# A hybrid decoder layer in float32: the long convolution as three filters on even and odd tokens, its sums of x by DMA, gates on half tiles, and another scheduling model

## The chip, the cores and the metric

The kernel runs on one core of one Trainium2 chip. The metric is the device time of one execution in microseconds, as the median of several runs. The engines named below are PE (TensorE, matmuls), DVE (VectorE), ACT (ScalarE), POOL (GpSimd) and SP (SyncE); POOL and SP serve here mainly to issue DMA transfers, each from a queue that works in order.

## What is computed

One layer over 1024 tokens of width 1024, all in float32. Cut to what matters:

```python
h = rms_norm(x, g_mix)
z = h @ w_in + b_in                       # 1024 x 7168
va, ga, xb, gb, sa, sb = split(z)         # 1024, 1024, 1536, 1536, 1024, 1024
u = va * sigmoid(ga)
u = causal_depthwise_conv(u, conv_a_w, conv_a_b)      # width 31
u = silu(layer_norm(u));  y_a = u @ w_a_out
v = causal_depthwise_conv(xb, conv_b_w, conv_b_b)     # width 4
r, i = sigmoid(block_diag(v, w_a)), sigmoid(block_diag(v, w_x))   # 16 heads of 96
v = linear_recurrence(exp(-8 r softplus(-lam)), ...)
y_b = (v * gelu(gb)) @ w_b_out
x = x + (sigmoid(sa) * y_a + sigmoid(sb) * y_b) @ w_o
x = x + square(relu(rms_norm(x, g_mlp) @ w_1)) @ w_2
out = rms_norm(x, g_final)
```

## The kernel before

Channels lie on the 128 partitions and tokens along the free dimension in the first stages. Each float32 product is made of three matmuls on operands split into a high part (a rounded copy, made by ACT) and a low part (the rest: made by a DVE subtraction, or, in `split_dma`, L64, by a negated copy on ACT and a DMA that adds the source to it, issued from POOL's queue). A 128 x 1024 tile of activations comes from the pool `acts` (`T`, 35 buffers).

*First stage.* Chunks of 128 output channels of `z` are made by `zchunk` (L377): two 512-token halves, 48 matmuls of 512 columns each, into a PSUM tile `ps` (three buffers of 128 x 1024). The order is fixed by the loop at L554: three `xb` chunks (`xb_chunk`, for the first four passes), then a `va` and a `ga` chunk (`va_pair`, chunks z0 to z7 and z8 to z15 in the trace), and after each chunk one step of the recurrence branch (`rnn_steps`). `xb_chunk` reads PSUM on ACT (L396) and makes the short convolution. `rnn_gates` (L436) makes two gate products of a head in one 128 x 1024 PSUM tile `ps2`, of which there is a single buffer, and ACT reads it with a sigmoid (L448). `va_pair` makes `u` from two PSUM tiles: sigmoid on ACT (L500), product on DVE (L501). `conv` (L505) is the long convolution of one chunk of `u`: a first product on ACT, then 30 `scalar_tensor_tensor` instructions on DVE, each of which adds one shifted tap to the same tile `acc`. The result is stored (`yd`) and summed into `ysum` for the layer norm: for chunk 0 by a copy on ACT (L521), afterwards on DVE (L523). The table `CONVS` says after which `va` pair a convolution is written: 0 to 4 in the first stage; 5 to 7 come in the z stage.

*Sums of x.* `x_sums` (L538), called twice (for column blocks `c2` 0 and 1), makes four differences of blocks of x for the Strassen-Winograd form of the next stage: four loads, four DVE subtractions, then for each a high copy on ACT (L550) and a low part on DVE (L552).

*z stage* (L569 to L697). The other 28 chunks of `z` (`gb`, `sa`, `sb`) are made in 14 pairs with seven products each (`zseq`: pairs of (i, p)), 12 matmuls a product, into PSUM banks `z_ia`, `b`, `e`, `f`. `z_lhs` makes the left operands `zo` (p = 7 and 3 on ACT and DVE; the others by `split_dma`), `z_step` the products and what reads them.

*Later.* The two output products `yb` and `ya` with the layer norm between (`layer_norm_steps`, taken at j = 1 and 4 of the `yb` loop), the products with the gates `sa` and `sb` (L777, L790), the output projection, and the MLP in Strassen-Winograd form. These stages are the same in both kernels but for the two lines shown below.

The order on each engine is set by a scheduler: it takes the instructions as written, with priorities (`tc.high_priority()`; the convolution's taps have the lowest, `-LOWP`), weighs them with a model of time, and writes one fixed order for each engine. Each engine then works strictly in that order and waits on semaphores. The stages inside `tc.manual_schedule` (the first chunks, the MLP) keep the order as written on ACT, DVE and PE.

Of the kernel before, what the change touches and what calls it, by code (L numbers as in the profile page):

```python
# [9 lines left out]
F32 = mybir.dt.float32  # L10
# [15 lines left out]
CONVS = {0: 0, 1: 1, 2: 2, 3: 3, 5: 4}  # L26
# [4 lines left out]
def trunk_kernel(ctx: ExitStack, tc: tile.TileContext, x, xt_in, vecs, w_in, w_a_out, w_b_out,  # L31
# [186 lines left out]
    def x_spread(hf):  # L218

        rb[hf] = rb["tile"][:, HALVES[hf]]  # L220
# [43 lines left out]
    c4 = sm[:, 7, :]  # L264

# [34 lines left out]
    with tc.manual_schedule(engines={mybir.EngineType.Activation, mybir.EngineType.DVE,  # L300
# [16 lines left out]
        rb["tile"] = PS("rb", "ps2")  # L317
# [47 lines left out]
        decay()  # L365

# [69 lines left out]
    def rnn_gates(n):  # L436
        g, hh = divmod(n, 4)
        vh, vl = parts.pop(n)
        gh, gl = gws[n]
        for gi in range(2):  # L440
            ps = PS(f"rg{n}_{gi}", "ps2")
            for hf in range(2):
                o, hs = ps[:HD, HALVES[hf]], HALVES[hf]
                nc.tensor.matmul(o, gh[:, gi, :], vh[:, hs], start=True, stop=False)
                nc.tensor.matmul(o, gl[:, gi, :], vh[:, hs], start=False, stop=False)
                nc.tensor.matmul(o, gh[:, gi, :], vl[:, hs], start=False, stop=True)  # L446
            a = H(f"g{n}_{gi}")
            nc.scalar.activation(a, ps[:HD, :], AF.Sigmoid, bias=(ba_c, bx_c)[gi][:, n:n + 1])  # L448
# [44 lines left out]
    def va_pair(j):  # L493
        psv = zchunk(VA + j)
        step()
        psg = zchunk(GA + j)
        step()
        u = T(f"u{j}")
        with tc.high_priority():
            nc.scalar.activation(u, psg, AF.Sigmoid, bias=bin_c[:, GA + j:GA + j + 1])  # L500
            nc.vector.scalar_tensor_tensor(u, psv, bin_c[:, VA + j:VA + j + 1], u,  # L501
                                           ALU.add, ALU.mult)
        ut[j] = u

    def conv(j):  # L505
        u = ut.pop(j)
        acc = T(f"y{j}")
# [5 lines left out]
        nc.scalar.activation(acc, u, AF.Identity, scale=tap(0), bias=cab_c[:, j:j + 1])  # L513
        with tc.high_priority(-LOWP):
            for d in range(1, WA):
                nc.vector.scalar_tensor_tensor(acc[:, d:S], u[:, 0:S - d], tap(d), acc[:, d:S],  # L516
                                               ALU.mult, ALU.add)
            nc.sync.dma_start(yd[j], acc)
            if j == 0:
                ysum.append(T("ysum"))  # L520
                nc.scalar.activation(ysum[0], acc, AF.Copy)  # L521
            else:
                nc.vector.tensor_tensor(ysum[0], ysum[0], acc, ALU.add)  # L523
# [13 lines left out]

    def x_sums(c2):  # L538
        q = {}
        for n, (hf, kk) in {12: (1, 0), 11: (0, 0), 22: (1, 1), 21: (0, 1)}.items():  # L540
            q[n] = T(f"xs{n}_{c2}")
            nc.sync.dma_start(q[n], xu[hf, 2 * kk + c2])
        sub = nc.vector.tensor_tensor
        sub(q[11], q[12], q[11], ALU.subtract)
        sub(q[12], q[22], q[12], ALU.subtract)
        sub(q[22], q[22], q[11], ALU.subtract)
        sub(q[21], q[21], q[22], ALU.subtract)
# [16 lines left out]
    for _ in rnn_it:  # L564
        pass
    x_sums(1)


# [118 lines left out]
    for n, (i, p) in enumerate(zseq):  # L687
# [8 lines left out]
        if p == 4 and i in (0, 2, 5):  # L696
            conv({0: 5, 2: 6, 5: 7}[i])  # L697
# [72 lines left out]
    for j in range(8):  # L770
# [7 lines left out]
        if j in (1, 4):  # L778
# [5 lines left out]
    for j in range(8):  # L784
# [5 lines left out]
        nc.vector.tensor_tensor(sa, ps, sa, ALU.mult)  # L790
# [653 lines left out]
```

## Time and profile before

| | |
|---|---|
| median of 3 runs | 1662.33 us (1661.87 to 1665.65) |
| the profiled execution, its own time | 1662.79 us |
| its span in the profile | 1661.0 us |
| mean granted clock of TensorE | 0.983 |
| PE, DVE, ACT, POOL busy | 96%, 70%, 52%, 12% of the span |
| DMA moved | 297.02 MB, mean 179 GB/s |

Busy time by slices of a fortieth of the span (41.5 us), in tenths:

```
PE   8979899997899999989999999999999999999997
DVE  6784999999989995325533224875555367888888
ACT  5537577672755655624453314664444457555552
PEclk9989899998899999999999999999999999999999
```

In the rows quoted below, "L516 DVE ... y<-u,vec,y 128x1009" names the line of the kernel, the engine, output and inputs by tile name, and shape; "[9.25 <-ACT xb L396]" is the time for which the engine stood idle before the instruction and what ended that wait; a line L92 is the helper `mm3`, which makes most matmuls, L66 to L68 the helper `split_dma`.

### The profile page before, as it was taken

The page shows a single profiled execution, that of the slowest core. Times are in us where ns is not written, and L with a number is a line of the kernel's source. Part 1 is how long each engine was busy: PE and PEld are TensorE (multiplying, and loading weights), DVE is VectorE, ACT ScalarE, POOL GpSimd, SP SyncE. Part 2 cuts the span into 40 slices and gives each one's busy share as a digit, 9 for nine tenths or more (in the row PEclk, how much of TensorE's full clock was granted, in tenths as well). Part 3 has the DMA queues.
Part 4 walks back from the last instruction along what each step waited for, and adds up shares of the span by engine and source line. Part 5 has one row for each costly group of instructions (what it writes and reads, how often), then busy time and mean ns, then how long its engine had stood idle before and what let it go on. Part 6 is the DMA issues. An engine that isn't in the chain of part 4 may idle for free.

```text
span 1661.0 us, 18664 instructions
## 1 busy us (share of the span) xinstructions
PE 1588.0 (96%) x6910; PEld 1291.0 (78%) x6910; DVE 1155.5 (70%) x1341; ACT 870.9 (52%) x1135; POOL 201.4 (12%) x268
## 2 busy tenths in 40 slices
PE   8979899997899999989999999999999999999997
PEld 6867677785677777868888888788888888888886
DVE  6784999999989995325533224875555367888888
ACT  5537577672755655624453314664444457555552
POOL 0000000000233333301121100000000001111110
PEclk9989899998899999999999999999999999999999
DMA  9657778765588777847577543442233478988862
GB/s 363 159 135 173 194 198 215 207 184 178 132 232 215 209 203 191 228 143 215 140 204 182 140 154 99 133 159 101 102 126 111 139 257 220 225 215 216 223 131 101
DMA packets 97130, 297.02 MB, mean 179 GB/s; under 512 B 11360, under 2 KB 12896, under 8 KB 97040
## 3 DMA queue, kind: packets, MB, share of 16 engines
q1 hardware_dynamic: 63408, 195.46, 35.3%
q0 software_dynamic: 33488, 100.12, 28.0%
q8 instruction: 54, 0.88, 0.2%
q14 instruction: 36, 0.29, 0.0%
q10 hardware_dynamic: 144, 0.26, 0.0%
HBM read 144.02 MB, written 54.53 MB: 120 GB/s over the span
## 4 chain that ended last, share of the span: by engine, by line
PE 73%; DVE 14%; DMA 6%; issue 4%; ACT 3%; POOL 0%; SPq 0%; DVEq 0%; POOLq 0%; ACTq 0%
PE d L1228 14%; PE yb L92 7%; DVE y L516 7%; PE z L92 6%; PE ya L92 5%; PE o L827 3%; PE e L1343 2%; PE keep L1228 2%; PE o L92 2%; DMA zo<-zw 2%; PE z L257 2%; DMA zo<-zs 1%; DVE g L474 1%; DMA hg<-hgd 1%; DVE v L404 1%
## 5 line engine op out<-in xcount | busy, mean ns | idle before, releaser
L516 DVE SCALAR_TENSOR_TENSOR y<-u,vec,y 128x1009 f32<-128x1009 f32 (+22 forms) x240 | 299.8, 1264 | 6.1 <-ACT y L513 2.6
L92 PE MATMUL z<-xh,win_h 128*128 128x512 f32 x400 | 127.2, 399 | 15.8 <-ACT xb L396 9.2
L92 PE MATMUL z<-xl,win_h 128*128 128x512 f32 x400 | 126.1, 396 | 0.0
L1240 DVE TENSOR_TENSOR acc<-acc,d 128x1024 f32<-128x1024 f32 x72 | 87.8, 1219 | 33.4 <-PE d L1228 32.7
L92 PEld LDWEIGHTS z<-xh,win_h 128*128 128x128 f32 x400 | 76.7, 193 | 34.1 <-ACT xb L396 9.7
L92 PE MATMUL z<-xh,win_l 128*128 128x512 f32 x400 | 94.8, 389 | 0.0
L92 PEld LDWEIGHTS z<-xl,win_h 128*128 128x128 f32 x400 | 76.8, 192 | 17.1
L92 PEld LDWEIGHTS z<-xh,win_l 128*128 128x128 f32 x400 | 75.1, 188 | 15.7
L67 POOL DMA_DIRECT2D win_l<-win_raw x25 | 21.7, 869 | 332.5 <-ACT win_l L66 273.5
L961 ACT ACTIVATE o<-s 128x512 fp32r<-128x512 f32 x64 | 38.1, 621 | 32.7 <-DVE s L953 28.5
L961 ACT ACTIVATE o<-w_raw 128x512 fp32r<-128x512 f32 x40 | 25.0, 624 | 51.2 <-DVE o L875 50.8
L404 DVE SCALAR_TENSOR_TENSOR v<-xb,vec,v 128x1023 f32<-128x1023 f32 (+2 forms) x36 | 45.6, 1277 | 8.8 <-ACT v L399 8.7
L68 ACT ACTIVATE win_h<-win_raw 128x1024 fp32r<-128x1024 f32 x25 | 26.3, 1056 | 43.7 <-PE z L92 37.3
L67 POOL DMA_DIRECT2D zo<-zw x42 | 37.1, 883 | 90.7 <-ACT zo L66 88.5
L448 ACT ACTIVATE g<-rg,vec 96x1024 f32<-96x1024 f32 x32 | 35.6, 1111 | 21.4 <-PE rg L446 14.6
L875 DVE TENSOR_TENSOR o<-s,o 128x512 fp32r<-128x512 f32 x64 | 42.4, 684 | 5.9 <-ACT o L961 5.8
L777 DVE TENSOR_TENSOR m<-yb,sb 128x1024 f32<-128x1024 f32 x8 | 9.8, 1222 | 52.7 <-PE yb L92 52.7
L859 DVE TENSOR_TENSOR x<-xr,o 128x1024 f32<-128x1024 f32 x8 | 9.6, 1218 | 52.2 <-PE o L827 37.7
L67 POOL DMA_DIRECT2D db_1l<-wr x7 | 6.1, 873 | 327.1 <-ACT db_1l L66 304.5
L790 DVE TENSOR_TENSOR sa<-ya,sa 128x1024 f32<-128x1024 f32 x8 | 9.8, 1225 | 43.9 <-PE ya L92 43.9
L118 ACT ACTIVATE xn<-x 128x1024 f32<-128x1024 f32 x8 | 8.5, 1057 | 58.8 <-DVE x L859 58.8
L92 PE MATMUL ya<-suh,wa_h 128*128 128x512 f32 x128 | 39.1, 389 | 0.0
(1577 smaller groups left out, 4599.1 us busy)
## 6 DMA issues: line engine op xcount, KB each, us to landing
fr<-fd SPq DMA_DIRECT2D x32, 512.0 KB, 5.7
wr<-in_w_dram SPq DMA_DIRECT2D x32, 512.0 KB, 5.9
w_raw<-in_w_dram SPq DMA_DIRECT2D x31, 512.0 KB, 3.7
zw<-in_w_in_dram SPq DMA_DIRECT2D x28, 512.0 KB, 4.7
win_raw<-in_w_in_dram SPq DMA_DIRECT2D x25, 512.0 KB, 4.9
win_l<-win_raw POOLq DMA_DIRECT2D x25, 512.0 KB, 4.8
zo<-zw POOLq DMA_DIRECT2D x42, 256.0 KB, 3.6
fd<-fa SPq DMA_DIRECT2D x16, 512.0 KB, 3.3
```

Source lines behind the costliest of these rows:

```text
L67: nc.gpsimd.dma_start(l, src, accum_op=ALU.add)
L92: nc.tensor.matmul(ps[:, HALVES[hf]], a, b[hf], start=i == 0, stop=i == len(todo) - 1)
L257: nc.tensor.matmul(z0[i][:, HALVES[hf]], w0[i][w][:, k, :], xpart(a, hf, k), start=k == 0 and which == "hh", stop=k == 7 and which == "hl" ...
L404: nc.vector.scalar_tensor_tensor(v[:, d:S], a[:, 0:S - d], cbw_c[:, w * 12 + t:w * 12 + t + 1], v[:, d:S], ALU.mult, ALU.add)
L448: nc.scalar.activation(a, ps[:HD, :], AF.Sigmoid, bias=(ba_c, bx_c)[gi][:, n:n + 1])
L516: nc.vector.scalar_tensor_tensor(acc[:, d:S], u[:, 0:S - d], tap(d), acc[:, d:S], ALU.mult, ALU.add)
L827: nc.tensor.matmul(ps[:, HALVES[hf]], tok(a, k, t), wo[k][b][:, HALVES[hf]], start=k == 0 and b == 0 and n == 0, stop=k == 7 and b == 1)
L875: tt(l, src, h.bitcast(F32), ALU.subtract)
L961: nc.scalar.activation(o[:, 0], src, AF.Copy)
L1228: nc.tensor.matmul(o, a, b, start=n == 0 and (p != 1 or g == 0), stop=n == len(todo) - 1, skip_group_check=p == 1 and g > 0)
L1240: tt(acc[p, q2], acc[p, q2], ps, ALU.add)
L1343: nc.tensor.matmul(o, a, b, start=n == 0, stop=n == len(todo) - 1)
```

## The change

1. *Convolution.* `u` is written with the even tokens in the first half and the odd tokens in the second. The 31 taps fall into an even filter (16 taps) and an odd one (15). The product of the two-phase filter is made of three filters on 512 tokens: the even taps on the even tokens (`p0`), the odd taps on the odd tokens (`p1`), and the sums of neighbouring taps (`csum`) on the sum of even and odd tokens (`p2`), from which `p0` and `p1` are then subtracted for the odd outputs; `p1`, shifted by one, is added to `p0` for the even outputs. `y` and `ysum` stay in that order; the product with `sa` puts `ya` back.
2. *Sums of x.* ACT negates a block in place and a DMA from POOL's queue adds the other block. `x_sums` is split into the sums and `x_parts`; the second call of the sums moves to j = 6.
3. *Gates.* Each half of a gate product has a PSUM tile of its own, one bank, two buffers; ACT reads each half with high priority. The 128 x 1024 tile with the tag `ps2` of the first pool goes.
4. *Places.* Convolutions 0 to 3 in the first stage (after pairs 0, 1, 2, 4), 4 to 7 in the z stage (after pairs 0, 1, 4, 7). `ysum`'s first copy moves to DVE. The first layer norm step is taken at j = 2.
5. *Scheduler.* The scheduler weighs the instructions with its other model of time (`schedule_with_timeline_sim`), so the order on every engine outside the manual stages can differ.

```diff
-CONVS = {0: 0, 1: 1, 2: 2, 3: 3, 5: 4}
+CONVS = {0: 0, 1: 1, 2: 2, 4: 3}
+    def PS2(name):
+        return pp.tile([P, HS], F32, tag="half", name=name, bufs=2)
...
+        nc.vector.tensor_scalar(cab2, cab_c, 2.0, None, ALU.mult)
+        pairs = caw[:, 8:].rearrange("p (i o j) -> p i o j", o=2, j=8)
+        nc.vector.tensor_tensor(csum, pairs[:, :, 0, :], pairs[:, :, 1, :], ALU.add)
...
-            ps = PS(f"rg{n}_{gi}", "ps2")
-            for hf in range(2):
-                o, hs = ps[:HD, HALVES[hf]], HALVES[hf]
+            a = H(f"g{n}_{gi}")
+            for hf, hs in enumerate(HALVES):
+                ps = PS2(f"rg{n}_{gi}{hf}")
+                o = ps[:HD, :]
...
-            nc.scalar.activation(a, ps[:HD, :], AF.Sigmoid, bias=(ba_c, bx_c)[gi][:, n:n + 1])
+                with tc.high_priority():
+                    nc.scalar.activation(a[:, hs], o, AF.Sigmoid,
+                                         bias=(ba_c, bx_c)[gi][:, n:n + 1])
...
+            uv = u.rearrange("p (o n) -> p o n", o=2)
+            nc.scalar.activation(uv, psg.rearrange("p (n o) -> p o n", o=2), AF.Sigmoid,
+                                 bias=bin_c[:, GA + j:GA + j + 1])
+            nc.vector.scalar_tensor_tensor(uv, psv.rearrange("p (n o) -> p o n", o=2),
+                                           bin_c[:, VA + j:VA + j + 1], uv, ALU.add, ALU.mult)
...
-        nc.scalar.activation(acc, u, AF.Identity, scale=tap(0), bias=cab_c[:, j:j + 1])
+        nc.scalar.activation(p0, xe, AF.Identity, scale=tap(0), bias=bias)
+        nc.scalar.activation(p1, xo, AF.Copy, scale=tap(1))
         with tc.high_priority(-LOWP):
-            for d in range(1, WA):
-                nc.vector.scalar_tensor_tensor(acc[:, d:S], u[:, 0:S - d], tap(d), acc[:, d:S],
-                                               ALU.mult, ALU.add)
+            nc.vector.tensor_tensor(xs, xe, xo, add)
+            nc.vector.tensor_scalar(p2, xs, taps(0), cab2[:, j:j + 1], ALU.mult, add)
+            for k in range(1, NE):
+                for o, a, c in ((p0, xe, tap(2 * k)), (p2, xs, taps(k)),
+                                (p1, xo, tap(2 * k + 1) if k < NE - 1 else None)):
+                    if c is not None:
+                        nc.vector.scalar_tensor_tensor(o[:, k:], a[:, 0:HS - k], c, o[:, k:],
+                                                       ALU.mult, add)
+            nc.vector.tensor_tensor(p2, p2, p0, sub)
+            nc.vector.tensor_tensor(p2, p2, p1, sub)
+            nc.vector.tensor_tensor(p0[:, 1:], p0[:, 1:], p1[:, 0:HS - 1], add)
             nc.sync.dma_start(yd[j], acc)
             if j == 0:
                 ysum.append(T("ysum"))
-                nc.scalar.activation(ysum[0], acc, AF.Copy)
+                nc.vector.tensor_copy(ysum[0], acc)
...
+        for n in (11, 12):
             q[n] = T(f"xs{n}_{c2}")
+            nc.sync.dma_start(q[n], blk[n])
+        for n, src, b in ((11, 11, 12), (12, 12, 22), (22, 11, 22), (21, 22, 21)):
+            if n not in q:
+                q[n] = T(f"xs{n}_{c2}")
+            nc.scalar.activation(q[n], q[src], AF.Copy, scale=-1.0)
+            nc.gpsimd.dma_start(q[n], blk[b], accum_op=ALU.add)
...
         if j == 5:
             x_sums(0)
-    for _ in rnn_it:
-        pass
-    x_sums(1)
+            x_parts(0)
+        elif j == 6:
+            for _ in rnn_it:
+                pass
+            x_sums(1)
+    x_parts(1)
...
-        if p == 4 and i in (0, 2, 5):
-            conv({0: 5, 2: 6, 5: 7}[i])
+        if p == 4 and i in (0, 1, 4, 7):
+            conv({0: 4, 1: 5, 4: 6, 7: 7}[i])
...
-        if j in (1, 4):
+        if j in (2, 4):
             next(ln_it, None)
...
-        nc.vector.tensor_tensor(sa, ps, sa, ALU.mult)
+        sav = sa.rearrange("p (n o) -> p o n", o=2)
+        nc.vector.tensor_tensor(sav, ps.rearrange("p (o n) -> p o n", o=2), sav, ALU.mult)
...
-    with _tile.TileContext(nc) as tc:
+    with _tile.TileContext(nc, schedule_with_timeline_sim=True) as tc:
```

More of the change, by code (lines that the diff above doesn't have):

```diff
@@ L218, in x_spread @@
     def x_spread(hf):
-        rb[hf] = rb["tile"][:, HALVES[hf]]
+        rb[hf] = PS2(f"rb{hf}")
         for i in range(4):
@@ L264, in trunk_kernel @@
     c4 = sm[:, 7, :]
+    csum = cp.tile([P, WA // 2, 8], F32, name="csum")
+    cab2 = cp.tile([P, 8], F32, name="cab2")
     def decay():
```

29 lines of the change are left out of this document (15 added, 14 removed).

## The prediction

> **What bounds the kernel now.** I read the page first, then busy time by stage, then the waits of PE, then the timelines around its longest waits, and the order in which each built program places its instructions on an engine. Page, busy shares:
>
> ```profile
> span 1661.0 us, 18664 instructions
> PE 1588.0 (96%) x6910; PEld 1291.0 (78%) x6910; DVE 1155.5 (70%) x1341; ACT 870.9 (52%) x1135; POOL 201.4 (12%) x268
> ```
>
> PE is busy for all but 73 us. The windows (busy time of an engine, instructions in brackets, then granted clock, DMA share and GB/s) say where those lie:
>
> ```profile
> 120.00:180.00 60.00, 53.54 (x206) 40.60 (x207) 35.05 (x33) 43.35 (x44) 2.61 (x3) 0.87 0.72 190
> 180.00:240.00 60.00, 60.00 (x264) 48.16 (x263) 58.16 (x53) 45.24 (x45) 3.48 (x4) 1.00 0.75 180
> 360.00:420.00 60.00, 43.63 (x174) 34.58 (x173) 59.57 (x52) 18.29 (x21) 3.15 (x4) 0.88 0.55 179
> 540.00:600.00 60.00, 58.30 (x256) 47.29 (x255) 56.79 (x63) 38.20 (x65) 20.02 (x27) 1.00 0.77 204
> 600.00:660.00 60.00, 55.41 (x232) 44.09 (x231) 41.95 (x46) 32.97 (x58) 18.95 (x26) 0.97 0.78 206
> 780.00:840.00 60.00, 60.00 (x263) 48.99 (x261) 29.80 (x21) 28.92 (x30) 9.73 (x13) 1.00 0.50 129
> ```
>
> A full window holds 264 matmuls (0.227 us each). From 780 on PE is full and the change touches little there, so those 880 us stay. What can be won lies before: the first stage (to 404 us) and the z stage (to some 710), where VectorE is full as well (59.57 of 60 at 360). A stop costs more than itself: in 120 to 180 PE was busy 53.54 us for 206 matmuls worth 46.8, at a clock of 0.87. The three stops that matter, as the timeline of PE has them:
>
> ```profile
> 120.12 1.22 PE L92 MATMUL z<-xh,win_h 128*128 128x512 f32 x2 [9.25 <-ACT xb L396]
> 169.43 0.74 PE L444 MATMUL rg<-vh,rgh 96*96 96x512 f32 x1 [5.14 <-ACT g L448]
> 391.10 1.22 PE L92 MATMUL z<-xh,win_h 128*128 128x512 f32 x2 [5.85 <-ACT u L500]
> ```
>
> **Part 1: the first sum `ysum` leaves ScalarE.** Timelines of ScalarE and VectorE (start, duration):
>
> ```profile
> 110.91 1.06 ACT L66 ACTIVATE win_l<-win_raw 128x1024 fp32r<-128x1024 f32 x1 [2.52 <-PE z L92]
> 118.01 1.06 ACT L521 ACTIVATE ysum<-y 128x1024 f32<-128x1024 f32 x1 [6.04 <-DVE y L516]
> 118.97 1.10 ACT L396 ACTIVATE xb<-z,vec 128x1024 f32<-128x1024 f32 x1
> 90.72 27.25 DVE L516 SCALAR_TENSOR_TENSOR y<-u,vec,y 128x1014 f32<-128x1014 f32 x21
> ```
>
> ScalarE works in order. The copy to `ysum` waits until VectorE's convolution 0 is done, and behind it stands the read of `xb` that frees the PSUM tile PE waits for. Now the copy is VectorE's; in the new order `xb` follows that win_l directly. It starts at 111.9 and ends at 113.0, and PE, which stopped at 120.12 - 9.25 = 110.87, stops 2.1 us: 7.1 won. The cold restart goes mostly too:
>
> ```profile
> 120.00:130.00 10.00, 9.88 (x31) 7.56 (x32) 7.52 (x7) 7.87 (x9) 0.00 (x0) 0.71 0.66 190
> 390.00:400.00 10.00, 8.90 (x30) 7.17 (x31) 9.89 (x9) 1.04 (x1) 0.00 (x0) 0.72 0.96 389
> ```
>
> 31 matmuls are worth 7.0 us and took 9.88: 2.8 lost here, of which I give back 2.4. Part 1: +9.5 (7.1 to 10).
>
> **Part 2: convolution as three filters.** What an instruction costs VectorE is its step to the next start, not its duration:
>
> ```profile
> 384.60 1.25 DVE L516 SCALAR_TENSOR_TENSOR y<-u,vec,y 128x994 f32<-128x994 f32 x1
> 385.77 1.22 DVE L547 TENSOR_TENSOR xs<-xs,xs 128x1024 f32<-128x1024 f32 x1
> 20.59 0.74 DVE L227 SCALAR_TENSOR_TENSOR xc<-xc,vec,rb 128x512 f32<-128x512 f32 x1
> 21.25 0.68 DVE L232 TENSOR_TENSOR xl<-xc,xh 128x512 fp32r<-128x512 f32 x1
> 21.86 0.74 DVE L227 SCALAR_TENSOR_TENSOR xc<-xc,vec,rb 128x512 f32<-128x512 f32 x1
> ```
>
> A tap followed by other work steps 1.17; in the chain above, each tap on the sum of the one before, 27.25 / 21 = 1.30. At 512 wide a tap steps 0.66 and a tensor_tensor 0.61. Before: 30 taps, 35 us interleaved to 39 in a chain. After: 15 + 15 + 14 = 44 taps on three sums in turn, so none waits for its neighbour, 44 x 0.655 = 28.8; xs, the first product and three closing additions 5 x 0.61 = 3.0; together 31.8. That is 3 to 7 us less each, and 8 fewer 1024-wide subtractions (part 4). No trace row has three sums in turn; bounds are 0.61 and the full 0.74 a tap (29.9 and 35.6 us). I take 0.655, the row of the same form.
>
> The Trainium skill, "VectorE: DVE Perf Modes", section "The DRAIN you can't avoid", speaks against this part: the next instruction starts only when the pipe has emptied, chaining cannot skip that, so the count of instructions should be kept low. By that rule a tap costs its whole 0.74 and a convolution 35.6, and almost nothing is won. The trace agrees for dependent taps only (a step of 1.30); an instruction that depends on nothing just written starts before the former has ended (1.17 against 1.25).
>
> What the time gains: between `u0` (first gated product) and `u7` the built orders hold 133 convolution instructions before, 165 us by the steps above (1.24 each), and 199 now, 133 us (0.67 each, the wide `ysum` among them). VectorE so has some 36 us of slack before `u7` (with part 4) and PE is the bound of the first stage: the gain is PE's stops, counted in the other parts, not these 36 us. Two short stops of 0.75 and 1.7 us behind late VectorE results I count at +1 (0 to 2.4).
>
> **Part 3: gates in halves.** PE's waits, in total, times, longest, and the forms:
>
> ```profile
> PE rg L444 <- ACT g L448: 7.1, 4, 5.1
> L448 ACT ACTIVATE g<-rg,vec 96x1024 f32<-96x1024 f32 x32 | 35.6, 1111 | 21.4 <-PE rg L446 14.6 <-DMA g<-g 5.9 <-ACT u L500 0.8
> L893 ACT ACTIVATE hq<-tr_m,vec 128x512 f32<-128x512 f32 x16 | 9.8, 695 | 0.0
> L448 ACT ACT_TABLE_LOAD x9 | 11.5, 1283 | 0.2
> ```
>
> 64 half reads at 0.695 are 44.5 us for 35.6: 9 more on ScalarE, which has 15 us free in 180 to 240. PE now waits for half a tile. But the long wait came of tables and scan work queued ahead of gate 4, and in the new order two tables, a root and a win_l (2 x 1.28 + 2 x 1.05) still stand between gates 3 and 4: about 3 us remain. +3 (-3 to +9, cold restart included).
>
> **Part 4: the sums of x by DMA.** Before, ScalarE's copies of the sums wait for VectorE, and `u6` waits behind them:
>
> ```profile
> 384.72 1.06 ACT L550 ACTIVATE xs6h<-xs 128x1024 fp32r<-128x1024 f32 x1 [9.25 <-DVE xs L546]
> 389.93 1.11 ACT L500 ACTIVATE u<-z,vec 128x1024 f32<-128x1024 f32 x1
> xs<-xu SPq DMA_DIRECT2D x8, 512.0 KB, 6.2
> win_l<-win_raw POOLq DMA_DIRECT2D x25, 512.0 KB, 4.8
> zo<-zs POOLq DMA_DIRECT2D x28, 256.0 KB, 3.8
> L67 POOL DMA_DIRECT2D zo<-zw x42 | 37.1, 883 | 90.7 <-ACT zo L66 88.5 <-PE z13f L637 1.4 <-issue 0.4
> ```
>
> This is the stop of 5.85 at 391.10, and 30 matmuls worth 6.8 took 8.9 after it: 8 us in all. Now a chain takes its place, on the same in-order ScalarE: load (6.2), negate (1), accumulate (0.9 to issue on POOL's queue, 4.8 to land), negate, accumulate, then the copies, then `u6`. Counted from the end of chunk z13, with the load issued 1 us before it: xs11 lands at 12, xs22 at 19, xs21 at 26, `u6` done at 28 and its VectorE part at 30. PE has z6, z14 and z7 in hand (3 x 48 x 0.227 = 32.7) before it needs that tile: the chain is covered by 3 us. Behind it on POOL's queue stand win7_l and win15_l, landing at 20 and 35 and wanted at 29 and 40. +8 (0 where landings take 2 us more).
>
> **Part 5: into the z stage.** Last matmuls of z15, `u7`, the low parts zo2_7 and, ten pairs later, zo12_7, and zo2_7's matmuls on the chain that ended last:
>
> ```profile
> 400.55 3.79 PE L92 MATMUL z<-xh,win_l 128*128 128x512 f32 x16
> 406.67 1.28 DVE L501 SCALAR_TENSOR_TENSOR u<-z,vec,u 128x1024 f32<-128x1024 f32 x1
> 450.88 0.69 DVE L617 TENSOR_TENSOR zo<-zs,zo 128x512 fp32r<-128x512 f32 x1
> 659.37 0.68 DVE L617 TENSOR_TENSOR zo<-zs,zo 128x512 fp32r<-128x512 f32 x1
> 459.03 2.72 PE z2f L637 x12
> ```
>
> Before, z15's end (404.3) to z2f is 54.7 us. After, ScalarE reaches zo0_1 behind the second chain, so PE stands some 8 us there where it stood 11 in several stops; but convolutions 4 and 5 now both sit ahead of zo2_7: 52 taps and the like (33 us), 4 wide subtractions (4.6) and 19 half-wide ones (11.6), 49 us against 16 x 1.19 + 8 x 1.14 + 11.6 = 40 before, which took 43. With the same 3.5 of waits z2f comes 57 us after z15. -2 (-8 to +8).
>
> The z stage itself: a pair takes (659.37 - 450.88) / 10 = 20.85 us before, where PE needs 7 x 12 x 0.227 = 19.1 and VectorE, with 8 to 12 half-wide instructions and 10 to 11 taps, 17 to 20; now it is 18 taps of 0.655, 17 to 19. But PE's stops go on after 600 us, where VectorE has slack. 0 (-20 to +15, rivals).
>
> **Part 6: strided reads.** Even and odd tokens are sorted as ScalarE and VectorE read PSUM; no row has such a read. Between no cost and as much again as an unstrided one (1.1 each, the `u` row above), only `u7`'s two lie on the path: -1 (-2 to 0). The closing products with `sa` hide under full PE. The Trainium skill, "SBUF — State Buffer", section "Door 1: The DMA port swizzle", has lines of 8 bytes in PSUM, two values, and a price for every crossing, which would be the doubling; no row here shows it.
>
> **Sum.** 9.5 + 1 + 3 + 8 - 2 + 0 - 1 = 18.5. The profiled execution took 1662.79 (span 1661.0), the median of the runs is 1662.33, so it stands for them: 1662.8 - 18.5 = 1644.
>
> **Rivals.** (a) *The z stage runs better too.* If less VectorE work brings 20.85 to 19.6 over 12 pairs, 15 more: 1629. For it: VectorE full until 600. Against it: the stops after. (b) *The new fixed order starves the z stage.* The built order puts zo_6's negation behind the z_b copy, itself behind the end of z_a; before it stood ahead. From a negation to PE's use:
>
> ```profile
> 545.61 0.63 ACT L66 ACTIVATE zo<-zw 128x512 fp32r<-128x512 f32 x1 [1.72 <-PE z6f L637]
> 552.66 0.73 PE L637 MATMUL z6a<-xh,zo 128*128 128x512 f32 x2 [1.70 <-DMA zo<-zw]
> ```
>
> That is 7.05 us, now begun 1.4 after z_a's end (two half-wide reads of 0.695), against 30 matmuls or 6.8 us that PE has in hand: 1.65 lost a pair, 20 over 12, and 4 more at zo1_6, which stands behind a read that waits for z0e: 1668. That is the point from which it decides; at a trip of 8 us it loses 2.6 a pair and gives 1644 + 31 + 4 = 1679. Against it: without a queue on POOL the trip is 0.6 + 0.9 + 3.8 = 5.3 us, and zo_2, late in this row, has two matmuls more of cover. (c) *The chain of part 4 is not covered.* With 2 to 3 us more a landing the 8 of part 4 and 6 to 8 at `u7` go: 1660, no change. (d) *A tap pays its whole 0.74:* 4 convolutions x 3.8 use up 15 of the 36 us of slack, and 52 x 0.085 = 4.4 come on the path in part 5: 1649. For it: chained taps do; against it: the steps of 0.66. It is what the Trainium skill's rule of part 2 would make. That the gates or filters do not do what they say I see no sign of: the built program holds the same 6873 matmuls.
>
> **How the numbers follow.** Forecast 0.52; (a) 0.17; (b) 0.14, a third of it short of 1668; (c) 0.08; (d) 0.09. A measurement here tells 0.3%, 5 us, from no change: faster means under 1657. Faster is the forecast less 0.02, (a) and (d): 0.76; slower two thirds of (b) and a little: 0.11; same the rest, 0.13. Range 1625 to 1668: (a) and the upper ends of parts 3 and 5 below, (b) up to 1668 above.
>
> **What would show it.** Part 1: no stop over 3 us near 111. Part 2: a convolution alone on VectorE in 31 to 33 us. Part 3: gate waits halved. Part 4: no wait of `xs6h` longer than its landing with PE stopped behind `u6`. Part 5: z2f 55 to 58 us after z15. It is wrong if PE's idle before 710 us has not fallen, or if waits for zo in the z stage exceed 20 us.

## The result: 16 us slower, and the profile after

The changed kernel takes 1678.2 us (median of 4 runs, 1676.91 to 1679.08) where the kernel before takes 1662.24 in the same comparison (4 runs): a ratio of 1.0091, 95% interval 1.0073 to 1.0108. The forecast was 1644. The profiled execution took 1677.35 us, with a span of 1675.6.

The page of the changed kernel, busy shares:

```profile
span 1675.6 us, 18924 instructions
PE 1588.4 (95%) x6910; PEld 1291.3 (77%) x6910; DVE 1114.5 (67%) x1488; ACT 886.3 (53%) x1184; POOL 205.9 (12%) x276
```

VectorE lost 41 us of work, as meant, and PE's work is the same to 0.4 us. So PE's idle time grew. The windows answer to those of before (busy time and instructions of PE, PEld, DVE, ACT, POOL, then granted clock, DMA share, GB/s):

```profile
120.00:180.00 60.00, 50.54 (x204) 38.19 (x203) 36.67 (x39) 47.75 (x56) 2.58 (x3) 0.89 0.77 210
180.00:240.00 60.00, 55.25 (x242) 43.97 (x241) 52.92 (x68) 43.19 (x49) 3.44 (x4) 1.00 0.61 149
360.00:420.00 60.00, 42.92 (x175) 34.08 (x174) 42.83 (x48) 29.09 (x31) 10.28 (x12) 0.87 0.86 226
540.00:600.00 60.00, 55.19 (x230) 43.66 (x229) 50.93 (x80) 36.34 (x62) 18.83 (x26) 0.97 0.76 203
```

VectorE is no longer full between 360 and 420 (42.83 where it had 59.57), and PE is no better off there: 42.92 for 43.63. From 180 to 240, where PE was full, it now does 242 matmuls instead of 264. So the amount of VectorE's work was not what held PE in these stages. The timeline of PE, its longest stops, and its waits in total (us, times, longest):

```profile
112.38 0.73 PE L95 MATMUL z<-xh,win_h 128*128 128x512 f32 x2 [2.15 <-ACT xb L403]
157.99 0.74 PE L452 MATMUL rg<-vh,rgh 96*96 96x512 f32 x1 [5.52 <-ACT g L456]
164.12 0.74 PE L452 MATMUL rg<-vh,rgh 96*96 96x512 f32 x1 [3.26 <-ACT g L456]
389.23 6.22 PE L95 MATMUL z<-xh,win_l 128*128 128x512 f32 x16 [3.97 <-DMA win_l<-win_raw]
419.50 0.79 PE L683 MATMUL z0a<-xh,zo 128*128 128x512 f32 x1 [12.89 <-ACT zo L71]
```

```profile
PE rg L452 <- ACT g L456: 18.6, 6, 5.5
PE z0a L683 <- ACT zo L71: 12.9, 1, 12.9
```

The stop of 9.25 at 120 us became 2.15, as forecast. In its place stand 18.6 us of waits at the gates (7.1 before) and 12.9 at the start of the z stage (3.8 before; from the end of z15 to z2f PE stands 19.9 us in all, for 12.8). Where the two executions part is read from the timelines of PE: the end of the last z15 matmul, and the first matmuls of z2f, yb and d (us from the start).

| | z15 ends | z2f | yb | ya ends | d | last work |
|---|---|---|---|---|---|---|
| before | 404.3 | 458.9 | 709.3 | 939.1 | 1347.7 | 1657.9 |
| after | 406.6 | 471.1 | 720.8 | 945.5 | 1353.8 | 1672.2 |

So 2.3 us are lost in the first stage and 9.2 more by the start of `yb`, all of them between the end of z15 and z2f (from there to `yb` it is 249.7 us for 250.5 before); 5.1 come back between yb and ya (1.8 of them at the waits for `hgh`; the rest I did not follow); and 8.2 are lost after d, in a stage that the prediction had taken as untouched. The last stage, after and then before (timelines of PE and VectorE: the stops of PE's last products, and the first and the last read of the last product `e`):

```profile
1615.25 0.49 PE L1390 MATMUL e<-lb11h,la21h 128*128 128x512 f32 x1 [1.39 <-ACT la21h L1170]
1617.87 0.50 PE L1275 MATMUL d<-db_4h,da_4h 128*128 128x512 f32 x1 [1.89 <-DVE acc L1287]
1631.34 1.28 DVE L1401 TENSOR_TENSOR y<-acc,e 128x512 f32<-128x512 f32 x2
1663.98 2.48 DVE L1401 TENSOR_TENSOR y<-acc,e 128x512 f32<-128x512 f32 x4 [0.55 <-PE e L1390]
```

```profile
1618.21 1.27 DVE L1354 TENSOR_TENSOR y<-acc,e 128x512 f32<-128x512 f32 x2
1652.64 0.69 DVE L1354 TENSOR_TENSOR y<-acc,e 128x512 f32<-128x512 f32 x1
```

Before, VectorE reads the first tile of `e` at 1618.2, between two folds of `acc`; now all but two of the 16 folds of both halves stand ahead of it in VectorE's order, the first read is 13 us later, PE stops twice, and four half reads are left over when PE is done. This code (`last_part`, `fold`, `finish`) did not change. It is written behind the manual stages of the MLP, so the scheduler places it, and its model of time is the only part of the change that reaches it.

### The profile page after: what moved, and what is told of

It reads as the page before. It is cut to its first block, busy times and chain, and to the rows that moved or that the text cites. A ratio compares the mean times of both kernels' runs of the same rounds, so it can differ in the third digit from the quotient of the medians.

```text
span 1675.6 us, 18924 instructions
## 1 busy us (share of the span) xinstructions
PE 1588.4 (95%) x6910; PEld 1291.3 (77%) x6910; DVE 1114.5 (67%) x1488; ACT 886.3 (53%) x1184; POOL 205.9 (12%) x276
## 4 chain that ended last, share of the span: by engine, by line
PE 62%; issue 11%; DMA 8%; ACT 4%; DVE 3%; POOL 1%; SPq 0%; POOLq 0%; ACTq 0%; DVEq 0%
PE d L1275 13%; PE ya L95 5%; PE yb L95 4%; PE o L874 3%; PE e L1390 3%; PE z L95 3%; PE keep L1275 2%; PE o L95 2%; DMA zo<-zs 2%; DMA zo<-zw 1%; DMA g<-g 1%; PE o L898 1%; DMA yn<-yd 1%; DMA win_l<-win_raw 1%; DMA wb2a_raw<-in_w_b_out_dram 1%
## 5 line engine op out<-in xcount | busy, mean ns | idle before, releaser
L95 PE MATMUL z<-xh,win_l 128*128 128x512 f32 x400 | 99.2, 401 | 4.0 <-DMA win_l<-win_raw 4.0
L548 DVE SCALAR_TENSOR_TENSOR y<-u,vec,y 128x498 f32<-128x498 f32 (+14 forms) x120 | 86.5, 740 | 0.3 <-ACT y L539 0.3
L548 DVE SCALAR_TENSOR_TENSOR yt<-u,vec,yt 128x499 f32<-128x499 f32 (+13 forms) x112 | 83.0, 741 | 0.0
L548 DVE SCALAR_TENSOR_TENSOR y<-yt,csum,y 128x499 f32<-128x499 f32 (+13 forms) x112 | 82.9, 740 | 0.0
L456 ACT ACTIVATE g<-rg,vec 96x512 f32<-96x512 f32 x64 | 41.3, 678 | 42.2 <-PE rg L454 17.3
L452 PE MATMUL rg<-vh,rgh 96*96 96x512 f32 x64 | 27.9, 435 | 18.7 <-ACT g L456 18.6
```

The costliest lines, as they stand in the source:

```text
L95: nc.tensor.matmul(ps[:, HALVES[hf]], a, b[hf], start=i == 0, stop=i == len(todo) - 1)
L456: nc.scalar.activation(a[:, hs], o, AF.Sigmoid, bias=(ba_c, bx_c)[gi][:, n:n + 1])
L548: nc.vector.scalar_tensor_tensor(o[:, k:], a[:, 0:HS - k], c, o[:, k:], ALU.mult, add)
```

## The experiments

All times are medians beside runs of the kernel before on the same chip (1662.1 to 1663.2 in these comparisons). A kernel's own runs spread over 3 to 16 us, so each ratio comes with its 95% interval; a difference of some 3 us between two of these kernels is at the limit of what they can tell.

Two theories came first. **T1**: the order that the scheduler's other model writes costs the time, and the parts themselves gain. **T2**: the parts cost it under any order.

### The model of time alone, the parts alone

The changed kernel with the old model, and the kernel before with the new one:

```diff
-    with _tile.TileContext(nc, schedule_with_timeline_sim=True) as tc:
+    with _tile.TileContext(nc) as tc:
```

> The changed kernel with everything but the scheduler's other model of time. Theory T1 (the order that the new model writes is what costs): the parts bring most of what was forecast, 1645 to 1655 us; ScalarE no longer keeps the read of u7 behind the last negation of the second chain of sums, PE's stop at z0a falls from 12.9 to under 5 us, and the last stage runs as before (8 us back). Theory T2 (the parts themselves cost it: the chain of sums by DMA on an in-order ScalarE, and halves of gates, under any order): only the last stage's 8 us come back, 1667 to 1672 us, with z0a still stopping for over 10 us.

> The kernel before with the scheduler's other model of time and nothing else. T1: slower, 1670 to 1680 us: 8 to 10 us in the last stage (PE's matmuls of the last product stop again and end 15 us later than before) and 4 us or more ahead of it. T2: the last stage's 8 us alone, 1668 to 1672, and nothing lost ahead of 700 us.

Measured: 1672.3 us for the parts under the old model (ratio 1.0064, 1.0052 to 1.0076) and 1697.4 for the new model alone (1.0202, 1.0189 to 1.0215). Both theories hold a part. The new model alone costs 34.5 us, more than either foresaw; from d to the end it takes 319.8 us against 310.2, and nearly three quarters of the loss lie ahead of that. Its window after z15 has VectorE full and PE at a clock of 0.80:

```profile
420.00:480.00 60.00, 44.89 (x164) 35.08 (x164) 60.00 (x62) 25.88 (x40) 8.12 (x11) 0.80 0.44 110
```

But the parts under the old model are 9.4 slower than the kernel before, too, though the last stage is back at 310.2, and PE still stands 13.5 us at z0a, as T2 said. So T1 alone falls.

Then the filters alone (the edits of `conv`, of `u`, of the product with `sa`, and `ysum` on VectorE; places, sums, gates and model as before), and the changed kernel with VectorE's sums of x:

> The kernel before with parts 1 and 2 alone (three filters, the first sum copied on VectorE), its own model of time and its own places of the convolutions. By the prediction's terms 9.5 and 1 us less, and up to 15 less in the z stage if VectorE bounds it: 1637 to 1652. If the filters bring nothing because PE bounds that stage: 1652. If neither (a tap at 512 wide pays its whole 0.74 us and VectorE is the bound from u7 on): 1655 to 1662.

```diff
-            nc.scalar.activation(q[n], q[src], AF.Copy, scale=-1.0)
-            nc.gpsimd.dma_start(q[n], blk[b], accum_op=ALU.add)
+        sub(q[11], q[12], q[11], ALU.subtract)
+        sub(q[12], q[22], q[12], ALU.subtract)
+        sub(q[22], q[22], q[11], ALU.subtract)
+        sub(q[21], q[21], q[22], ALU.subtract)
```

> The changed kernel with the sums of x formed by VectorE as before (no chain of accumulating DMAs) and all else as changed, the new model of time too. T1: the model still places the work badly, 1670 to 1680. T2: the stop of 12.9 us at z0a goes and VectorE gets 8 wide subtractions back, 1662 to 1669, with u7 read right after z15 ends.

Measured: 1663.6 (1.0006, 0.9995 to 1.0016), so parts 1 and 2 bring nothing, which is slower than every expectation (the highest ended at 1662); and 1675.0 (1.0071, 1.0059 to 1.0083), 3 less than the changed kernel, with intervals that overlap. That second run is as T1 said and not as T2 said. In it the read of `u7` comes right behind z15 (404.1 us), and PE stands at the start of the z stage all the same:

```profile
412.05 0.79 PE L672 MATMUL z0a<-xh,zo 128*128 128x512 f32 x1 [8.01 <-ACT zo L71]
421.71 0.79 PE L672 MATMUL z1a<-xh,zo 128*128 128x512 f32 x1 [8.01 <-ACT zo L71]
450.49 0.80 PE L672 MATMUL z1b<-xs6h,zo 128*128 128x512 f32 x1 [4.91 <-ACT zo L71]
```

### Where the gain of part 1 goes

In the filters-alone kernel the stop at 120 is gone. Its timeline of PE has another, and behind it stand its window from 140 to 175 us and the groups of table loads on ScalarE in that window:

```profile
170.91 0.74 PE L449 MATMUL rg<-vh,rgh 96*96 96x512 f32 x1 [13.65 <-ACT g L453]
```

```profile
140.00:175.00 35.00, 20.15 (x82) 14.83 (x81) 17.20 (x17) 31.76 (x30) 1.74 (x2) 0.79 0.64 167
```

```profile
L469 ACT ACT_TABLE_LOAD x3 | 3.8, 1283 | 0.1
L453 ACT ACT_TABLE_LOAD x3 | 3.8, 1283 | 0.1
L473 ACT ACT_TABLE_LOAD x2 | 2.6, 1283 | 0.0
L470 ACT ACT_TABLE_LOAD x1 | 1.3, 1283 | 0.0
```

PE comes to gate 4 earlier by what part 1 won and waits there 13.65 us instead of 5.14, until the same moment as before (170.9; 169.4 before). ScalarE is busy 31.76 of 35 us: the exponentials, tanh and roots of the first group of scans, between gates, with nine loads of function tables, 11.5 us. This made theory **W**, a wall at ScalarE's scans. Its first test is part 1 alone, its second the halves of the gates, its third gates by tanh, so that gate, exponential and tanh need one table; beside them the sums by DMA on the filters-alone kernel.

```diff
-                nc.scalar.activation(ysum[0], acc, AF.Copy)
+                nc.vector.tensor_copy(ysum[0], acc)
```

> The kernel before with only the first sum of y copied by VectorE instead of ScalarE (part 1 alone). The prediction's part 1: the stop of 9.25 us at 120 us falls to about 2 and 7 to 10 us are won: 1652 to 1655. Theory W, a wall at ScalarE's first group of scans and gates (140 to 170 us, with the loads of its function tables): PE comes to gate 4 earlier by what was won and waits there for the same end, the stop at 169 us grows from 5.1 to 11 us or more, 1660 to 1665.

> The filters-alone kernel with the gates' products in two halves as in the change, under the old model of time. The prediction's part 3: 3 us less, 1658 to 1662. Theory W: halves do not shorten ScalarE's queue and the order has more switches between tables (33 table loads between 100 and 420 us without halves), so the stops move but their sum does not fall: 1664 to 1672.

```diff
-            nc.scalar.activation(a, ps[:HD, :], AF.Sigmoid, bias=(ba_c, bx_c)[gi][:, n:n + 1])
+            nc.scalar.activation(a, ps[:HD, :], AF.Tanh, scale=0.5,
+                                 bias=bh[:, 16 * gi + n:16 * gi + n + 1])
```

> The filters-alone kernel with the gates computed by tanh of half the argument (the factors of a half go into the decay's scales, the root's scale and the product with v; the result is the same function), so that a gate, an exponential and a tanh need one function table. Theory W with tables as the cost: of 33 table loads between 100 and 420 us some 10 to 16 remain, of the 9 between 110 and 185 us 4 or fewer, the stop of 13.65 us at gate 4 falls to 4 to 8, and the time to 1648 to 1657. Rival: the wall is the chain of data (gates, their moves by DMA, the scans), not the tables: the stop stays over 10 and the time 1660 to 1665.

> The filters-alone kernel with the sums of x by negation and accumulating DMA, as in the change (halves, new places and new model left out). The prediction's part 4: 8 us less, 1653 to 1657. Theory T2: the chain on in-order ScalarE holds up u6 or u7 and the first low parts of the z stage; more than it saves, 1667 to 1675, with z15 ending no earlier and z2f 5 to 10 us later than the filters alone (460.7 us).

Part 1 alone: 1670.3 (1.0040, 1.0025 to 1.0054), slower than W said, and W had the place wrong too: the stop at gate 4 is 5.46 us, as before, not 11 or more. The stop at 120 does fall to 2.15, and 12 us later a new one stands, behind ScalarE's gate read, which itself waits for the transfers that empty its buffer:

```profile
112.05 0.72 PE L92 MATMUL z<-xh,win_h 128*128 128x512 f32 x2 [2.15 <-ACT xb L396]
124.89 0.74 PE L444 MATMUL rg<-vh,rgh 96*96 96x512 f32 x1 [6.86 <-ACT g L448]
123.73 1.11 ACT L448 ACTIVATE g<-rg,vec 96x1024 f32<-96x1024 f32 x1 [8.51 <-DMA g<-g]
```

That one takes back what was won. The waits at the gates are 18.5 us in all (7.1 before), and z15 ends 8 us later than before.

Halves on the filters: 1667.1 (1.0024, 1.0012 to 1.0036), 3.5 slower than without them by the medians where the prediction gave 3 faster. Its gate waits shrink, and its longest stop in the first stage is now the read of `u` behind them (a longer one, 16.9 us, stands at z0a):

```profile
180.40 1.22 PE L95 MATMUL z<-xh,win_h 128*128 128x512 f32 x2 [10.28 <-ACT u L511]
```

Gates by tanh: 1663.3 (1.0004, 0.9994 to 1.0015), no gain. The roots still switch tables: 26 loads between 100 and 420 us for 33, not the 10 to 16 expected, and the stop at gate 4 fell only to 10.21 (in a profiled execution of 1671.8 us, 8.5 above the median). The test was too weak.

Sums by DMA: 1667.8 (1.0022, 1.0008 to 1.0036), 4.2 slower by the medians where the prediction gave 8 faster. ScalarE's chain, and PE behind it:

```profile
398.49 1.06 ACT L581 ACTIVATE xs<-xs 128x1024 f32<-128x1024 f32 x1 [9.77 <-DMA xs<-xu]
407.80 1.11 ACT L507 ACTIVATE u<-z,vec 128x1024 f32<-128x1024 f32 x1
408.97 1.22 PE L92 MATMUL z<-xh,win_h 128*128 128x512 f32 x2 [14.42 <-ACT u L507]
```

The read of `u6` stands behind a negation that waits 9.77 us for an accumulating transfer, then four copies, of which the last waits again; PE stops 14.42.

### Take away the tables, not the wait

The scans are entered two gate steps later, so that the three tiles of a group are there and their exponentials, tanh and roots run one kind after the other. The built order then holds 25 table loads for 42.

```diff
-            if n >= 0 and n % 4 == 3:
-                rnn_scan(n // 4)
+            if n > 3 and n % 4 == 1:
+                rnn_scan(n // 4 - 1)
             yield
+        rnn_scan(3)
```

This on the filters, on the kernel before, and on the changed kernel under the old model; beside them the new places of the convolutions alone.

> The filters-alone kernel with each group's scan entered two gate steps later, so that its three tiles are all there and ScalarE does the exponentials, tanh and roots of a group in one run: the built order holds 25 table loads instead of 42. Theory W with tables: the stop of 13.65 us at gate 4 falls under 5, z15 ends 5 us or more before the 408.2 of the filters alone, 1648 to 1658. Rival, the wall is the data of the gates (their moves by DMA): the stop stays over 9, 1660 to 1666. Rival, the place after z15 gives it back (z0a or z2f wait for the last sums of x and for u7 on VectorE): the stop falls, z15 ends earlier, and z2f is where it was, 459 to 465.

> The kernel before with each group's scan entered two gate steps later and nothing else (35 table loads in the built order become 25). Theory W: its stop of 5.14 us at gate 4 goes, but not the one of 9.25 at 120, so 3 to 8 us are won: 1655 to 1660. Rival (what is won in the first stage is given back after z15): 1661 to 1666.

> The changed kernel under the old model of time (1672 us), with the late scans (28 table loads in the built order). Theory W: 8 us or more less, 1658 to 1665, its stops of 4 and 5.9 at gates 4 and 5 and of 9.7 at 180 us under 5 together. Rival: 1668 to 1674, with the end of z15 earlier than 418.7 and the stop at z0a longer.

> The kernel before with only the new places of the convolutions (0, 1, 2, 4 in the first stage, four in the z stage). No work is added or taken away; one more convolution of 35 to 39 us lies in the z stage. If VectorE bounds the start of the z stage: 10 us or more slower, 1672 to 1685, z2f over 470. If the z stage has room: 1660 to 1668.

On the filters: 1660.3 (0.9989, 0.9977 to 1.0001). The stop of 13.65 is gone; ScalarE is busy 18.57 of the 35 us and PE 32.85:

```profile
159.65 0.47 PE L449 MATMUL rg<-vh,rgh 96*96 96x512 f32 x1 [1.99 <-ACT rgh L52]
```

```profile
140.00:175.00 35.00, 32.85 (x136) 24.99 (x135) 18.09 (x22) 18.57 (x20) 1.74 (x2) 0.95 0.81 203
```

That shows the wall: 12.7 us of PE's time in this stretch hung on where ScalarE does the scans' functions. The run does not part the two things that the edit does: the loads are fewer, and the whole group now runs later, from 175 us on, so that no load of a table lies in this stretch. On the changed kernel under the old model it is worth 10.1 (1662.2 for 1672.3; ratio to before 1.0003, 0.9989 to 1.0017), the whole 9.4 that the parts had lost. On the kernel before it costs 2.7 (1664.9; 1.0020, 1.0010 to 1.0031), a miss of W: the stop of 5.14 goes, that of 9.27 stays, and z15 ends 7 us later. The new places cost nothing (1660.3; 0.9989, 0.9975 to 1.0002).

But on the filters only 3.3 of the 12.7 us reached the end, and z15 ended 2.9 earlier where W asked for 5. Most of the gain is lost before z15, in one place. PE comes there 17 us ahead of the filters alone: as many matmuls of the first stage are done at 323.9 us as there at 341.3. The window from 325 to 345 us in the filters alone, and then with the late scans:

```profile
325.00:345.00 20.00, 19.50 (x85) 15.60 (x86) 20.00 (x32) 8.21 (x9) 0.87 (x1) 1.00 0.89 215
```

```profile
325.00:345.00 20.00, 13.51 (x39) 8.54 (x38) 20.00 (x23) 13.24 (x14) 0.87 (x1) 0.67 0.68 202
```

With the late scans PE does 46 matmuls less in this window, 10.4 us of its work at 0.227 each. It stops four times, for 1.2 to 2.2 us, behind reads of gates and of `u`, and the granted clock is 0.67. The late scans on the kernel before lose as much between 325 and 360 us. Of the runs with late scans on the filters only the two with halves do more here (76 and 78 matmuls), and they lose it again at other stops.

Behind z15 PE waits as before:

```profile
409.46 0.47 PE L669 MATMUL z0a<-xh,zo 128*128 128x512 f32 x1 [4.25 <-DVE u L510]
421.10 0.80 PE L669 MATMUL z1a<-xh,zo 128*128 128x512 f32 x1 [6.50 <-ACT zo L68]
418.00 1.06 ACT L582 ACTIVATE xs6h<-xs 128x1024 fp32r<-128x1024 f32 x1 [10.60 <-DVE xs L578]
```

ScalarE waits 10.6 us for the second sums of x, which stand between a convolution's taps in VectorE's fixed order; the weights of z1a, which need none of it, stand behind that copy. Theory **R**: the start of the z stage is a second wall (by the windows above, not the only one left).

### Take away the second wall

The loads of the second sums of x are issued after u6 instead of after u7:

```diff
         if j == 5:
+            x_loads(0)
             x_sums(0)
+        if j == 6:
+            x_loads(1)
```

With filters, late scans and new places (VectorE's sums of x, whole gates and the old model of time); the same without the filters and with the first sum on ScalarE; the first kernel without the early loads:

> Filters, the new places of the convolutions and late scans under the old model of time, VectorE's sums of x, and the loads of the second sums of x issued after u6 instead of after u7: in the built order their four subtractions then stand ahead of u7 on VectorE and no tap stands between u7 and the split of the sums. Theory R (what the first stage wins is waited for after z15: for u7 and for the sums of x behind taps on VectorE, and for ScalarE's copies of them): the stops from z15's end to the second bank (4.25 and 6.5 us with the late scans alone) fall under 6 together, z2f comes within 50 us of z15's end (52.8 there) and the time is 1650 to 1656. Rival (the z stage is bound by something else, its trips by DMA): z2f moves with z15's end by no more than 2 us and the time is 1657 to 1662.

> The same without the filters and with the first sum of y on ScalarE: new places, late scans and early loads on the kernel before. If the filters are worth what the prediction's parts 1 and 2 gave them once ScalarE's tables are out of the way, this one is 8 us or more slower than with them, 1660 to 1668. If they are worth nothing, it is the same within 3 us.

> Filters, new places and late scans without the early loads: parts the effect of the loads from that of the places. Theory R: 1655 to 1661, the stops at z0a and the second bank over 9 us together. Rival: as with the early loads within 2 us.

Measured: 1652.1 (0.9941, 0.9928 to 0.9954), 1661.5 (0.9995, 0.9982 to 1.0008) and 1659.7 (0.9982, 0.9965 to 0.9998). The first beats both kernels; z15 ends at 397.9 and z2f comes at 448.0, 50.1 us later (54.5 before, 64.4 after). The early loads are worth 7.6 us. The filters, with the first sum on VectorE, worth nothing on the kernel before, are worth 9.3 here, where the prediction's parts 1 and 2 gave 10.5; how much of it is the stop of 9.25 at 120, which stands in the kernel without them, the runs do not part. The place at 325 to 345 us is as bad in the best kernel as with the late scans alone (36 matmuls, clock 0.67). One thing of R missed: one stop remains, now 11.3 us in a piece, behind a copy on ScalarE that waits for a buffer:

```profile
409.20 0.80 PE L677 MATMUL z0a<-xh,zo 128*128 128x512 f32 x1 [11.32 <-ACT zo L68]
407.57 1.06 ACT L587 ACTIVATE xs4h<-xs 128x1024 fp32r<-128x1024 f32 x1 [5.18 <-DVE xs7l L589]
```

Last, that copy behind the first weights of the z stage (`x_parts(1)` written after the first four `z_lhs`), the halves, and the new model, each on the 1652 us kernel:

> The kernel with filters, late scans and early loads (1652 us), with ScalarE's copies of the second sums of x entered behind the first four weights of the z stage: in the built order both parts of zo0_1 then stand ahead of xs4h, which waited 5.2 us there. Theory R: the stop of 11.3 us at z0a falls to 5 to 7, 1645 to 1650. Rival (PE is caught up later in the z stage): z2f no earlier than 446, 1650 to 1654.

> The same kernel (1652 us, without the later copies) with the gates in halves. The prediction's part 3 gives 3 us less: 1647 to 1650. If halves only add to ScalarE (64 reads for 32 and 4 more table loads in the built order, 28 for 24: some 10 us of work beside PE) and the long waits were of the tables: the same or slower, 1652 to 1658.

> The same kernel (1652 us) with the scheduler's other model of time and nothing else. Theory T1 for the last stage: from the first matmul of d to the end 318 to 320 us instead of 310, and more before it (35 table loads in the built order for 24): 1662 to 1680. If the new model only disturbs what the old order had tuned: 1652 to 1658.

Measured: 1653.1 (0.9941, 0.9926 to 0.9955), 1657.8 (0.9971, 0.9959 to 0.9983) and 1677.4 (1.0092, 1.0075 to 1.0108). In the first the stop falls to 6.91 and 2.69 us at z0a and z1a, but z2f comes at 449.8 and yb at 700.0 (448.0 and 700.2): the z stage takes it back, as the rival said. What holds it there I have not found. Halves cost 5.7 us. The new model costs 25.2: from d to the end 320.9 us for 310.3, and ahead of it 35 table loads in the built order for 24, with the waits at the gates back (17.7 and 9.7 us):

```profile
PE rg L449 <- ACT g L453: 17.7, 7, 5.7
PE rg L449 <- ACT u L508: 9.7, 1, 9.7
```

## Why the prediction was wrong, point by point

Terms that were to win 18.5 us won nothing. Parts 1 and 2 together left the time as it was, the new places too, and the halves and the sums by DMA each cost some 3 to 4 us. Together, under the old model, the parts cost 9.4 us, and the late scans give that back whole. The new model adds 5.9 by the medians: 8.2 us in the last stage, with some won back ahead of it. These figures do not add up exactly, as the parts meet in the same places.

**What bounds the kernel: wrong in two places.** "From 780 on PE is full and the change touches little there, so those 880 us stay" failed: the last stage lost 8.2 us to the new model. In all four kernels with it d to the end takes 318.4 to 320.9 us, in all others 310.2 or 310.3. I had read part 5 as something that moves the changed stages; it rewrites every stage that is not manual, and I compared the built orders only up to the z stage. And "VectorE is full as well" was taken for a bound: with 41 us less on it PE gained nothing, since PE's long stops stand behind single results that come late in a fixed order.

**Part 1: +9.5 forecast; the local reading right, the sum wrong.** The stop is 2.15 us where 2.1 was forecast. The step that failed is "7.1 won": I did not ask what PE meets next. It meets gates whose reads come at a time that ScalarE's scans and the gates' transfers set: 18.5 us of waits at the gates, with part 1 alone as with the filters, for 7.1 before. Alone it cost 7.4 us; the traces show where the gain went, and not the whole of that cost.

**Part 2: the instruction costs right.** The timeline of VectorE after, convolution 0:

```profile
77.03 0.74 DVE L548 SCALAR_TENSOR_TENSOR y<-u,vec,y 128x511 f32<-128x511 f32 x1
77.69 0.75 DVE L548 SCALAR_TENSOR_TENSOR y<-yt,csum,y 128x511 f32<-128x511 f32 x1
108.28 0.69 DVE L556 COPY ysum<-y 128x1024 f32<-128x1024 f32 x1
```

A tap steps 0.66 (forecast 0.655) and the convolution takes 32.4 us from 75.8 (forecast 31.8), with one other instruction in it. So rival (d) falls. It stood on the rule of the Trainium skill ("VectorE: DVE Perf Modes", "The DRAIN you can't avoid") as I had put it. The same section adds that an instruction that is not held starts earlier; these rows are that case: on three sums in turn a tap starts 0.66 after one that lasts 0.74.

**Part 3: +3 forecast, -3.5 and -5.7 measured** (the first by medians whose intervals overlap a little, the second clear of noise). "About 3 us remain" of the wait at gate 4 failed: in the changed kernel PE stands 5.5 us at 158 and 3.3 at 164, and 18.6 at all gates. I counted two tables between gates 3 and 4, but PE, earlier by part 1, now waited for all of them, and halves double the reads. The Trainium skill ("ScalarE: Activation LUTs", "Table sets: the hidden batching unit") says to do all calls of one set before switching. The late scans are in line with it: 33 loads between 100 and 420 us become 16, and 13.65 us of stop become 1.99, though the scans also run later there.

**Part 4: +8 forecast, -4.2 measured** on the filters by the medians (and 3 dearer than VectorE's sums in the changed kernel, within the intervals). "The chain is covered by 3 us" failed on the landings: the forecast had 0.9 to issue and 4.8 to land. The 4.8 was the row of `win_l`, which adds a tile that is on the chip; the sums add blocks of `xu` from the main memory (DRAM). Median landings after (last number), and the timeline of ScalarE:

```profile
win_l<-win_raw POOLq DMA_DIRECT2D x25, 512.0 KB, 4.9
xs<-xu POOLq DMA_DIRECT2D x8, 512.0 KB, 7.6
```

```profile
404.60 1.06 ACT L585 ACTIVATE xs<-xs 128x1024 f32<-128x1024 f32 x1 [6.37 <-DMA xs<-xu]
414.46 1.06 ACT L585 ACTIVATE xs<-xs 128x1024 f32<-128x1024 f32 x1 [8.80 <-DMA xs<-xu]
415.42 1.10 ACT L511 ACTIVATE u<-z,vec 128x1024 f32<-128x1024 f32 x1
418.83 0.62 ACT L71 ACTIVATE zo<-zw 128x512 fp32r<-128x512 f32 x1
```

In two other runs with the chain the median of its landings is 6.3 and 8.2. From one negation's end (405.66) to the next's start is 8.8 us, where the forecast had 5.7. In the sums by DMA alone this shows ahead of u6, as the stop of 14.42. In the changed kernel the first chain was nearly covered: PE's stop of 3.97 at 389 waits for a `win_l` issued in the middle of the chain. The second chain keeps u7's read, due when z15 ends at 406.6, until 415.4, and the weights of z0a behind that. That is the condition of rival (c), 2 to 3 us more a landing; I gave it 0.08.

**Part 5: -2 forecast; z2f came 64.4 us after z15, not 57.** The step that failed is the 8 us that I gave PE to stand at z0a: it stood 12.9, and 2.9 and 3.7 more at z1. The second chain stands in front of z0a here, but it is not what the stretch hangs on. With VectorE's sums and no chain, under the same model, z2f comes 66.2 us after z15; in the kernel before with the new model alone, 63.8 (54.5 before); with the chain under the old model, 52.9. So it goes with the order that the new model writes, though on the 1652 us kernel that model makes it only 54.7 from 50.1. (2.5 us of the 64.4 and of the 66.2 are z2f's own place: 11 matmuls more stand ahead of it in PE's order.) Which instruction of the new order holds PE once the chain is gone, the runs do not show. The convolutions, which my sum of 49 us on VectorE went by, were not it: the new places alone cost nothing. "The z stage itself: 0" was out by little: from z2f to `yb` 249.7 us for 250.5.

**Part 6: forecast -1, nothing seen.** The group of VectorE's reads of PSUM after and before:

```profile
L513 DVE SCALAR_TENSOR_TENSOR u<-z,vec,u 128x1024 f32<-128x1024 f32 x8 | 10.2, 1280 | 19.7 <-ACT u L511 19.7
```

```profile
L501 DVE SCALAR_TENSOR_TENSOR u<-z,vec,u 128x1024 f32<-128x1024 f32 x8 | 10.2, 1275 | 5.9 <-ACT u L500 5.9
```

1280 ns for 1275, and ScalarE's read of `u` takes 1.10 us for 1.11 (rows of part 4, here and in the prediction): no doubling, so the price that the prediction named for crossing lines in PSUM does not show in these reads.

**Rivals and marks.** (b) gave 1668 to 1679 for a fixed order that starves the z stage. That the time falls in its range is luck: its place, the negations behind `z_b`, cost nothing on balance, since PE's waits for `zo` behind z2f are 11.6 us for 11.4 before. The gates, the start of the z stage and the last stage are what cost. Of the two marks of a wrong forecast one was met: PE's idle time between 60 us and yb went from 49.5 to 57.8 us. The other said nothing: PE's waits for `zo` in the z stage are over 20 us (31.3), but they were 20.5 in the kernel before.

## What to carry to other kernels

A stop of the bounding engine is worth what its removal gives only up to the next result that the engine will need: name that result and when it is due, as if the stop were gone, before counting the gain. An option of a scheduler changes every stage that it plans, so its orders are to be compared to the last instruction. Less work on the fullest side engine (the filters) brought nothing alone, 1663.6 us, and neither did moving cheap steps (three tiles' functions in one run, a load issued a chunk earlier, another place for a convolution), 1661.5 us; both together brought 1652.1.

## What the runs showed that I had not expected

Loads of function tables: 1283 ns each, up to nine in 35 us of ScalarE. An accumulating transfer of 512 KB from the main memory that a chain waits for: 8.8 us between two negations and a median landing of 7.6, where one that adds a tile on the chip landed in 4.9. And a change of one line on the kernel before (part 1 alone) that removes 7 us of stop and costs 7.4. And a gain that was 17 us of PE's work at 324 us and 3 at the end of the same stage.
